# Interleaving two tensors: which queue opens with which load, and a tiny first write left out

## The chip, the cores and the metric

The kernel runs on one core of a Trainium2 chip. The metric is the time of one execution on the device, in microseconds (us); of several runs the median is taken. A hardware profile of one execution stands beside the times.

## The reference

The inputs x and y are float32 tensors of 32 x 256 x 1024, 33.5 MB each. The output has twice as many elements in its last dimension: x at the even places, y at the odd ones.

```python
result = np.zeros((batch, seq, dim * 2), dtype=np.float32)
result[..., 0::2] = x
result[..., 1::2] = y
```

Nothing is calculated. 67.1 MB have to be read and 67.1 MB to be written.

## The kernel before, in words

All three tensors are taken as flat arrays. The inputs are cut into eight pieces of 128 x 8192 elements (`WL = 8192`), so a piece of x or y is 4.19 MB, 32 KB in each of the 128 partitions of SBUF. For each piece the loop at L50 loads an x tile (L56) and a y tile (L57), both issued from SyncE (SP). Then, for each half of the piece (`WS = 4096` columns, the loop at L60), VectorE copies the half of x into the even columns of an output tile (L70) and the half of y into its odd columns (L71). The output tile, 128 x 8192 elements and again 4.19 MB, is stored by a DMA that ScalarE (ACT) issues (L72). So there are 16 loads of 4.19 MB, 32 copies and 16 stores of 4.19 MB.

The pools for x, y and output tiles have two buffers each (L35 to L37). A load of piece k+2 waits until the copies out of piece k are done; a copy into an output tile waits until the store from two before has landed. The waits and the order on each engine are made by the tile framework.

Two queues carry the DMAs: the profile calls SP's q1 and ACT's q10. Before, q1 holds all loads and q10 all stores. DMAs of a queue are taken in order of issue.

Two things concern the opening. At L44 to L47 a zero tile of 16 x 128 elements is made by VectorE and written by ACT to 16 places in the output that the first store overwrites later. And after compiling, L86 to L104 take the first DMA that SP issues (the load of the first x tile) out of the body and put it into the program's first block, ahead of SP's drain, with which the opening barrier of the engines begins. Every other DMA is issued after that barrier.

In what follows x0 and y0 are the tiles of the first piece, x1 and y1 those of the second, and so on.

Of the kernel before, what the change touches and what calls it, by code (L numbers as in the profile page):

```python
# [2 lines left out]

# [4 lines left out]


@with_exitstack
def _interleave(
    ctx: ExitStack,
    tc: tile.TileContext,
    x: bass.AP,
    y: bass.AP,
    out: bass.AP,
):
    nc = tc.nc
    P = 128  # L20

    total = 1
    for s in x.shape:
        total *= s

    WL = 8192
    WS = 4096

    xf = x.rearrange("b s d -> (b s d)")
    yf = y.rearrange("b s d -> (b s d)")  # L30
    of = out.rearrange("b s d -> (b s d)")

    fp32 = mybir.dt.float32

    xpool = ctx.enter_context(tc.tile_pool(name="xp", bufs=2))  # L35
    ypool = ctx.enter_context(tc.tile_pool(name="yp", bufs=2))
    opool = ctx.enter_context(tc.tile_pool(name="op", bufs=2))  # L37

    lwidths = [WL] * (total // P // WL)
    assert sum(lwidths) == total // P  # L40


    wpool = ctx.enter_context(tc.tile_pool(name="wp", bufs=1))
    zero = wpool.tile([16, 128], fp32, name="zero")  # L44
    nc.vector.memset(zero, 0.0)  # L45
    first = dataclasses.replace(of, offset=0, ap=[[2 * WL, 16], [1, 128]])
    nc.scalar.dma_start(out=first, in_=zero)  # L47

    start = 0
    for lw in lwidths:  # L50
        xtile = xpool.tile([P, WL], fp32, name="xtile")[:, :lw]
        ytile = ypool.tile([P, WL], fp32, name="ytile")[:, :lw]

        xs = dataclasses.replace(xf, offset=start, ap=[[lw, P], [1, lw]])
        ys = dataclasses.replace(yf, offset=start, ap=[[lw, P], [1, lw]])
        nc.sync.dma_start(out=xtile, in_=xs)  # L56
        nc.sync.dma_start(out=ytile, in_=ys)  # L57

        soff = 0
        while soff < lw:  # L60
            width = min(WS, lw - soff)
            otile = opool.tile([P, 2 * WS], fp32, name="otile")[:, : 2 * width]
            os_ = dataclasses.replace(
                of,
                offset=2 * start + 2 * soff,
                ap=[[2 * lw, P], [1, 2 * width]],
            )
            xsub = xtile[:, soff : soff + width]
            ysub = ytile[:, soff : soff + width]
            nc.vector.tensor_copy(out=otile[:, 0::2], in_=xsub)  # L70
            nc.vector.tensor_copy(out=otile[:, 1::2], in_=ysub)  # L71
            nc.scalar.dma_start(out=os_, in_=otile)  # L72
            soff += width

        start += P * lw
    assert start == total


def kernel(tc, x, y, out):
    nc = tc.nc  # L80
    _interleave(tc, x, y, out)
    tc.close()
    tc.compile()  # L83


    blocks = nc.main_func.blocks  # L86
    opening = blocks[0].instructions
    at, moved = next(
        (b, i)
        for b in blocks[1:]  # L90
        for i in b.instructions
        if i.engine == mybir.EngineType.SP and i.opcode == "DMACopy"
    )
    assert not moved.sync_info.on_wait
    body = at.instructions
    body.remove(moved)
    gate = next(
        n
        for n, i in enumerate(opening)
        if i.engine == mybir.EngineType.SP and i.opcode == "Drain"  # L100
    )
    opening.insert(gate, moved)
    at.instructions = body
    blocks[0].instructions = opening  # L104


# [1 line left out]
_INS = ['x', 'y']  # L108
_OUTS = [((32, 256, 2048), 'float32')]


# [23 lines left out]
```

## Time and profile before

| | |
|---|---|
| Median of 3 runs | 315.92 us (315.55 to 316.17) |
| Time of the profiled execution | 315.62 us |
| Span in its profile | 313.8 us |
| VectorE busy | 72.8 us (23%) |
| Moved | 134.23 MB, mean 428 GB/s |
| Loads on q1, stores on q10 | 67.11 MB, 67.12 MB |

The span runs from the first to the last instruction; 1.8 us of the execution lie around it. "Busy" counts VectorE's and GpSimd's work, not the issuing of DMAs. A group's line in the profile has the line of the kernel, the engine and operation, the tiles, the count, then busy time and mean time of one, then how long the engine stood idle before and what ended the wait. A line of the timeline has start, duration, engine, line and operation; where several are merged ("x3"), the duration runs from the first to the last. A line of the windows has the stretch, its length, busy time of VectorE and GpSimd, a clock that is of no use here, the busy share of the 16 DMA engines, and GB/s. The trace also has a record of every DMA packet, with its start, duration and size; a data packet of a tile is one row of 32 KB.

### The profile page before, as it was taken

The numbers are of one execution on the slowest core, as the hardware profiler recorded it, in microseconds if no ns is written. First come the engines' busy times: TensorE is split into PE (matmuls) and PEld (weight loads), VectorE is DVE, ScalarE is ACT, GpSimd is POOL, SyncE is SP. The second block draws the span as 40 slices with busy tenths as digits, with TensorE's granted clock in tenths as the row PEclk, the third lists the DMA queues.
The fourth block names the chain that finished last, engine by engine and source line by source line (L and its number), as shares of the span: only waits on it lengthen the run. The fifth ranks groups of instructions, "written<-read, shape, count | busy, mean of one in ns | idle before, by whom it ended". The sixth has DMA issues, their size and how long they took to land.

```text
span 313.8 us, 152 instructions
## 1 busy us (share of the span) xinstructions
DVE 72.8 (23%) x33; POOL 0.2 (0%) x4
## 2 busy tenths in 40 slices
DVE  0433002231032410325003150130501305023500
POOL 0000000000000000000000000000000000000000
DMA  8999999999999999999999999999999999999997
GB/s 339 464 405 397 468 401 464 405 464 405 464 405 464 405 459 409 451 418 451 418 434 434 430 439 426 443 413 455 401 468 401 468 401 468 401 468 401 464 405 334
DMA packets 4640, 134.23 MB, mean 428 GB/s; under 512 B 528, under 2 KB 544, under 8 KB 544
## 3 DMA queue, kind: packets, MB, share of 16 engines
q1 hardware_dynamic: 2304, 67.11, 49.9%
q10 hardware_dynamic: 2336, 67.12, 49.5%
HBM read 67.11 MB, written 67.12 MB: 428 GB/s over the span
## 4 chain that ended last, share of the span: by engine, by line
DMA 83%; DVE 11%; DVEq 1%; issue 0%
DMA out_dram<-otile 76%; DMA ytile<-in_y_dram 7%; DVE otile L71 6%; DVE otile L70 5%; DVEq L83 1%; DVEq L70 0%
## 5 line engine op out<-in xcount | busy, mean ns | idle before, releaser
L70 DVE COPY otile<-xtile 128x4096 f32<-128x4096 f32 x16 | 36.6, 2295 | 184.9 <-DMA out_dram<-otile 173.7
L71 DVE COPY otile<-ytile 128x4096 f32<-128x4096 f32 x16 | 36.6, 2292 | 39.8 <-DMA ytile<-in_y_dram 39.8
L45 DVE MEMSET zero<- 16x128 f32 x1 | 0.2, 165 | 0.9 <-PEq L119 0.9
L119 POOL MEMSET const-bfloat16-1.0<- 128x1 bf16 x1 | 0.1, 102 | 0.0
L119 POOL MEMSET const-uint8-127<- 128x1 uint8 x1 | 0.1, 102 | 0.0
L119 POOL MEMSET const-float32-0.0<- 128x1 f32 x1 | 0.1, 99 | 0.2 <-issue 0.2
L119 POOL MEMSET const-float32-1.0<- 128x1 f32 x1 | 0.1, 99 | 0.0
## 6 DMA issues: line engine op xcount, KB each, us to landing
out_dram<-otile ACTq DMA_DIRECT2D x16, 4096.0 KB, 29.1
xtile<-in_x_dram SPq DMA_DIRECT2D x8, 4096.0 KB, 43.6
ytile<-in_y_dram SPq DMA_DIRECT2D x8, 4096.0 KB, 60.7
out_dram<-zero ACTq DMA_DIRECT2D x1, 8.0 KB, 6.3
```

The costliest lines, as they stand in the source:

```text
L45: nc.vector.memset(zero, 0.0)
L70: nc.vector.tensor_copy(out=otile[:, 0::2], in_=xsub)
L71: nc.vector.tensor_copy(out=otile[:, 1::2], in_=ysub)
L83: tc.compile()
L119: nc = _bacc.Bacc("TRN2", target_bir_lowering=False, num_devices=1)
```

## The change

The zero tile, its memset and its write are gone. y0 is issued from ACT instead of SP. At the first turn of the loop the loads of the second piece are issued too: x1 from SP, the half of y1 in partitions 0 to 63 from ACT, and the half in partitions 64 to 127 from SP. The second turn finds its tiles in `held` and issues no loads. So q1 opens with x0, x1 and half of y1; q10 opens with y0 and the other half of y1, and the stores come after those. All later loads are on SP, all stores on ACT, as before.

The move ahead of the barrier is done for both engines: the first DMA of SP (x0) and the first of ACT (y0) go ahead of the drain of their engine. The rest of the diff writes the same copies and stores in another form.

```diff
-    wpool = ctx.enter_context(tc.tile_pool(name="wp", bufs=1))
-    zero = wpool.tile([16, 128], fp32, name="zero")
-    nc.vector.memset(zero, 0.0)
-    first = dataclasses.replace(of, offset=0, ap=[[2 * WL, 16], [1, 128]])
-    nc.scalar.dma_start(out=first, in_=zero)
+    def rows(flat, at, width, count=P):
+        return dataclasses.replace(flat, offset=at, ap=[[width, count], [1, width]])
...
+    held = None
+    for t, lw in enumerate(lwidths):
+        if held is None:
+            xtile = xpool.tile([P, WL], fp32, name="xtile")
+            ytile = ypool.tile([P, WL], fp32, name="ytile")
+        else:
+            xtile, ytile = held
+            held = None
...
+        if t != 1:
+            nc.sync.dma_start(out=xtile, in_=rows(xf, start, lw))
+            yq = nc.scalar if t == 0 else nc.sync
+            yq.dma_start(out=ytile, in_=rows(yf, start, lw))
+        if t == 0:
+            nxt = start + P * lw
+            nx = xpool.tile([P, WL], fp32, name="xtile")
+            ny = ypool.tile([P, WL], fp32, name="ytile")
+            nc.sync.dma_start(out=nx, in_=rows(xf, nxt, lw))
+            nc.scalar.dma_start(out=ny[:H], in_=rows(yf, nxt, lw, H))
+            nc.sync.dma_start(out=ny[H:], in_=rows(yf, nxt + H * lw, lw, P - H))
+            held = nx, ny
...
-    opening = blocks[0].instructions
-    at, moved = next(
-        (b, i)
-        for b in blocks[1:]
-        for i in b.instructions
-        if i.engine == mybir.EngineType.SP and i.opcode == "DMACopy"
-    )
...
+    for engine in (mybir.EngineType.SP, mybir.EngineType.Activation):
+        opening = blocks[0].instructions
+        at, moved = next(
+            (b, i)
+            for b in blocks[1:]
+            for i in b.instructions
+            if i.engine == engine and i.opcode == "DMACopy"
+        )
...
+            if i.engine == engine and i.opcode == "Drain"
```

More of the change, by code (lines that the diff above doesn't have):

```diff
@@ L40, in _interleave @@
     assert sum(lwidths) == total // P
-    wpool = ctx.enter_context(tc.tile_pool(name="wp", bufs=1))
-    zero = wpool.tile([16, 128], fp32, name="zero")
-    nc.vector.memset(zero, 0.0)
-    first = dataclasses.replace(of, offset=0, ap=[[2 * WL, 16], [1, 128]])
-    nc.scalar.dma_start(out=first, in_=zero)
-    start = 0
[L50 to L62, printed above, removed]
+    H = P // 2
+    def rows(flat, at, width, count=P):
+        return dataclasses.replace(flat, offset=at, ap=[[width, count], [1, width]])
+    start = 0
+    held = None
[18 more added lines that the diff above has]
+            held = nx, ny
+        for soff in range(0, lw, WS):
+            otile = opool.tile([P, 2 * WS], fp32, name="otile")
             os_ = dataclasses.replace(
@@ L65, in _interleave @@
                 offset=2 * start + 2 * soff,
-                ap=[[2 * lw, P], [1, 2 * width]],
+                ap=[[2 * lw, P], [1, 2 * WS]],
             )
[L68 to L71, printed above, removed]
+            nc.vector.tensor_copy(
+                out=otile[:, 0::2], in_=xtile[:, soff : soff + WS]
+            )
+            nc.vector.tensor_copy(
+                out=otile[:, 1::2], in_=ytile[:, soff : soff + WS]
+            )
             nc.scalar.dma_start(out=os_, in_=otile)
-            soff += width
         start += P * lw
@@ L86 @@
     blocks = nc.main_func.blocks
-    opening = blocks[0].instructions
-    at, moved = next(
-        (b, i)
-        for b in blocks[1:]
-        for i in b.instructions
-        if i.engine == mybir.EngineType.SP and i.opcode == "DMACopy"
-    )
[L94 to L104, printed above, removed]
+    for engine in (mybir.EngineType.SP, mybir.EngineType.Activation):
[5 more added lines that the diff above has]
+            if i.engine == engine and i.opcode == "DMACopy"
+        )
+        assert not moved.sync_info.on_wait
+        body = at.instructions
+        body.remove(moved)
+        gate = next(
+            n
+            for n, i in enumerate(opening)
+            if i.engine == engine and i.opcode == "Drain"
+        )
+        opening.insert(gate, moved)
+        at.instructions = body
+        blocks[0].instructions = opening
 _INS = ['x', 'y']
```

## The prediction

> **What bounds the kernel now.** First the page: busy time, the row of DMA shares, the queues, the groups.
>
> ```profile
> DVE 72.8 (23%) x33; POOL 0.2 (0%) x4
> ...
> DMA  8999999999999999999999999999999999999997
> ...
> DMA packets 4640, 134.23 MB, mean 428 GB/s; under 512 B 528, under 2 KB 544, under 8 KB 544
> ...
> q1 hardware_dynamic: 2304, 67.11, 49.9%
> q10 hardware_dynamic: 2336, 67.12, 49.5%
> ...
> L70 DVE COPY otile<-xtile 128x4096 f32<-128x4096 f32 x16 | 36.6, 2295 | 184.9 <-DMA out_dram<-otile 173.7
> L71 DVE COPY otile<-ytile 128x4096 f32<-128x4096 f32 x16 | 36.6, 2292 | 39.8 <-DMA ytile<-in_y_dram 39.8
> ```
>
> VectorE works 23% of the span; the 16 DMA engines are busy in every slice but the edges. VectorE waits 173.7 us for stores, so the chain of waits names stores (76%). But those stores wait for the DMA engines, which share their time between q1 (SP, loads) and q10 (ACT, stores). Next the timeline of the opening, to see who feeds them:
>
> ```profile
> 0.00 0.37 SPq L56 DMA_DIRECT2D xtile<-in_x_dram  x1
> ...
> 0.78 0.33 SPq L57 DMA_DIRECT2D ytile<-in_y_dram  x1
> 0.86 0.17 DVE L45 MEMSET zero<- 16x128 f32 x1 [0.86 <-PEq L119]
> 1.06 0.42 ACTq L47 DMA_DIRECT2D out_dram<-zero  x1
> 1.16 0.42 SPq L56 DMA_DIRECT2D xtile<-in_x_dram  x1
> 1.63 0.51 SPq L57 DMA_DIRECT2D ytile<-in_y_dram  x1
> 12.28 4.50 DVE L70 COPY otile<-xtile 128x4096 f32<-128x4096 f32 x2 [11.25 <-DMA xtile<-in_x_dram]
> 16.80 0.33 SPq L56 DMA_DIRECT2D xtile<-in_x_dram  x1
> 22.00 4.50 DVE L71 COPY otile<-ytile 128x4096 f32<-128x4096 f32 x2 [5.22 <-DMA ytile<-in_y_dram]
> 24.32 33.66 ACTq L72 DMA_DIRECT2D out_dram<-otile  x3
> ```
>
> By 2.14 us four loads (16.8 MB) stand in q1. x0 releases VectorE at 12.28, y0 at 22.00: 9.72 us for one 4.19 MB tile, with one queue at work, is 432 GB/s. One queue alone fills the engines. Last, windows, for where the rate falls short:
>
> ```profile
> 0.00:4.00 4.00, 0.17 (x1) 0.20 (x4) 1.00 0.78 262
> 4.00:24.00 20.00, 6.50 (x3) 0.00 (x0) 1.00 1.03 444
> 24.00:32.00 8.00, 2.50 (x2) 0.00 (x0) 1.00 1.00 397
> 32.00:288.00 256.00, 57.15 (x26) 0.00 (x0) 1.00 1.00 432
> 288.00:312.00 24.00, 6.47 (x3) 0.00 (x0) 1.00 1.01 437
> ```
>
> The last column is GB/s, the one before it the DMA share. The engines are busy throughout; the rate sags in two places only, the first 4 us and 24 to 32 us. (A window counts a packet where it starts, so edges wobble.) The packet records say what a slot is: a row of 32 KB takes 1.213 us on one engine. A 128-row tile is 8 rows on each of 16 engines, so the whole is 8x2 loads and 16 stores of 8 rows: 256 slots, 256 x 1.213 = 310.5 us. The first packet starts at 0.99 and needs 2.05 us (median of 16), so the cadence starts in effect at 1.84; 1.84 + 310.5 = 312.4. The last record ends at 312.71. The difference is the second sag: load packets in flight between 25.9 and 29.1, just ahead of the first big store's, take up to 1.9 us instead of 1.21. From rates spread evenly over each record (406.7 and 390.4 GB/s in the two 4 us windows from 24, against 433.3) it is (26.6 + 42.9) x 4 / 433.3 = 0.64 us. After the last packet come 1.14 us to the span's end at 313.85, and 1.77 us lie around the span (315.62). So time is won or lost only by idle slots, longer slots, or the two sags.
>
> [...] 433 GB/s with q1 alone, with both, and with q10 alone. [...] No 64-row transfer is in this trace. [...]
>
> **The change, part by part.**
>
> *y0 goes from SP's queue to ACT's, and both x0 and y0 are issued ahead of the barrier.* Rows of the two queues alternate, so x0 and y0 both end after some 16 slots: 1.84 + 16 x 1.213 = 21.2 us, plus about 0.7 us to release (x0 before: 11.54 to 12.28), some 21.9, as y0 does now (22.00). The early x0 copies are lost: VectorE does four copies of 2.3 us after 21 us, the first store leaves between 25.5 and 28 us instead of at 24.32. Nothing idles meanwhile: with y1's first half, q10 holds 12 slots a engine and q1 20. Cost 0; the cover is those 32 slots (38.8 us, until about 40). ACT's issue (0.4 us) ahead of its drain may hold the barrier a little and with it x1's issue (now 1.16); 16 slots, 19.4 us, are queued by then. POOL's queue has only its four constants. Cost 0.
>
> *The tiny write and its memset go.* One 512 B packet of 0.027 us on each engine, and VectorE's 0.17 us, which nothing waits for: gain 0.03 us. What it may have done for the first store is a rival below. The count of transfers stays 33, since y1 becomes two.
>
> *ACT's queue order.* y0 and half of y1 stand ahead of the stores. They wait for nothing. q10 has 12 rows an engine ahead of store 0, which ends them at slot 24: 1.84 + 29.1 = 30.9 us. The store's descriptors, issued by 28, then follow others in the same ring instead of opening it at 29.1. If the 0.64 us sag is the price of opening the ring, it goes or hides in the opening; if it belongs to the first large write, it stays. Between 0 and -0.64; I take half, -0.32.
>
> *SP's queue.* x1, then y1's second half, 20 slots, drain at about slot 40 (50 us); x2 is issued when x0's copies are done, before 28 us, y2 before 31. Neither queue runs dry. Later each store pair alternates as before: a store lands, two copies take 4.6 us, and the other store has 9.7 us or more to run. Cost 0.
>
> *y1 in two halves of 64 partitions.* The unknown. [...] The upper half-tile in q1 or the lower in q10, each has four slots an engine. First half (partitions 0 to 63), alternating with x1's rows: [...] +4 x 1.213 = 4.85 us, in any phase. Second half, alternating with store rows, which read SBUF: [...] +4 x (1.213 - offset between them). In perfect opposition that is 0. But the engines march nearly in step (store rows start within 0.43 us, at 29.10 to 29.53)[...]; I take 0.05 us, so 4 x 1.163 = 4.65. Sum 9.50. Bounds 0 (no limit) and 9.70; I take 9.50[...]. DMA slots are the path that sets the end, so all of it arrives there.
>
> Sum on the profiled execution: 315.62 + 9.50 - 0.32 - 0.03 = 324.77. The runs' median is 0.30 above this execution, so 325.1.
>
> **The rivals.** *Even slots, sag stays* (a tile half costs nothing, or its rows go to eight engines each, in balance; the sag is the first write's): 315.92 - 0.03 = 315.9, no change. For it: all records but those two groups are 1.213 us. [...] *Even slots, sag gone:* 315.92 - 0.64 - 0.03 = 315.25, faster. This is the case on the other side: its place is 25.9 to 29.1 us, its price 0.64 us, and it decides if a 64-row slot takes under 1.213 + 0.64/8 = 1.29 us and ring opening causes the sag. For it: only packets just ahead of q10's first large ones are long, and no later switch of queues costs anything. Against: the tiny write opened q10 at 5.27 with load rows beside it still at 1.213. *A colder first store:* the tiny write paid something for the first HBM write, and without it the store's first rows take what x0's took, +0.84 us: 316.8, slower. For it: x0's opening packets. Against: the sag occurs despite the tiny write.
>
> **How the numbers follow.** [...] 0.54 (own range 320.1 to 326.0: 315.92 + 4.85 - 0.64 to 315.92 + 9.70 + 0.4), even slots with the sag 0.18, without it 0.18, a colder store 0.10. A change under 0.2% (0.63 us) can't be told from none here. Slower 0.64, same 0.18, faster 0.18. Likeliest 325.1; the range, 315.1 to 326.0, reaches over all four, since leaving out the fast two would leave out 0.36.
>
> **What would show it.** Right: between some 21 and 31 us, and again between 45 and 60, the rate in the windows falls to about two thirds of 433 GB/s, and half-tile packets take near 2.4 us; later windows stay at 432; the last load ends some 9 us later; VectorE's first copies start near 21 us and DMA never idles. Wrong: half-tile rows at 1.21 us and a span within 1 us of 313.8; then the window 24 to 32 tells which rival holds. Idle DMA after 50 us would refute the queue count.

## The result, and the profile after

| | before | after |
|---|---|---|
| Median of 6 runs each, us | 316.02 (315.55 to 316.50) | 325.14 (324.81 to 325.88) |
| Profiled execution, us | 315.62 | 325.32 |
| Its span, us | 313.8 | 323.5 |
| Start to end of all data packets, us | 0.99 to 312.71 | 1.02 to 322.39 |

The changed kernel takes 1.029 of the time of the kernel before (95% interval 1.0275 to 1.0305). 9.7 us are added in the profiled executions, and almost all of it (9.65 us) lies between the first and the last packet.

From the page of the changed kernel, busy time, packets, queues and groups:

```profile
DVE 71.9 (22%) x32; POOL 0.2 (0%) x4
...
DMA  9999999999999999999999999999999999999997
...
DMA packets 4624, 134.22 MB, mean 415 GB/s; under 512 B 528, under 2 KB 528, under 8 KB 528
...
q10 hardware_dynamic: 2528, 73.40, 54.0%
q1 hardware_dynamic: 2096, 60.82, 45.4%
...
L79 DVE COPY otile<-xtile 128x4096 f32<-128x4096 f32 x16 | 36.7, 2295 | 236.1 <-DMA out_dram<-otile 169.9
```

The bytes and the copies are the same, and the DMA engines are as busy as before, in every slice, yet the mean rate is 415 GB/s instead of 428. Engines that are as busy and move less have rows that take longer. ACT's queue, q10, now carries 73.40 MB instead of 67.12, the 6.29 MB of y0 and half of y1.

The timeline of the opening of the changed kernel shows that what was moved went where it was meant to:

```profile
0.00 0.37 SPq L60 DMA_DIRECT2D xtile<-in_x_dram  x1
0.11 0.38 ACTq L62 DMA_DIRECT2D ytile<-in_y_dram  x1
...
0.92 0.33 SPq L67 DMA_DIRECT2D xtile<-in_x_dram  x1
0.92 0.51 ACTq L68 DMA_DIRECT2D ytile<-in_y_dram  x1
1.29 0.54 SPq L69 DMA_DIRECT2D ytile<-in_y_dram  x1
21.72 2.29 DVE L79 COPY otile<-xtile 128x4096 f32<-128x4096 f32 x1 [21.72 <-DMA xtile<-in_x_dram]
...
26.25 40.44 ACTq L85 DMA_DIRECT2D out_dram<-otile  x3
```

The barrier costs nothing: SP's first DMA behind it leaves at 0.92 instead of 0.78, but that is now x1, which before was the second and left at 1.16. VectorE starts at 21.72 instead of 12.28, the first store leaves at 26.25 instead of 24.32, and neither leaves the DMA engines idle. In both queues the DMAs land in the order in which they were issued: on SP x0 at 21.70, x1 at 46.44 and y1's upper half at 61.50; on ACT y0 at 21.87, y1's lower half at 39.13 and the first store at 61.69. In the opening the rows of the two queues alternate in waves of 16, which begin at 1.02 (SP), 2.78 (ACT), 4.00 (SP) and 5.20 us (ACT).

Windows of the changed kernel, cut where its rate changes (last column GB/s):

```profile
4.00:20.00 16.00, 0.00 (x0) 0.00 (x0) 1.00 1.03 444
22.00:38.00 16.00, 8.62 (x4) 0.00 (x0) 1.00 1.01 262
38.00:46.00 8.00, 0.00 (x0) 0.00 (x0) 1.00 1.07 459
46.00:60.00 14.00, 0.00 (x0) 0.00 (x0) 1.00 0.98 307
60.00:300.00 240.00, 58.46 (x26) 0.00 (x0) 1.00 1.00 433
```

and the same windows of the kernel before, but for the first:

```profile
22.00:38.00 16.00, 4.50 (x2) 0.00 (x0) 1.00 1.03 426
38.00:46.00 8.00, 0.00 (x0) 0.00 (x0) 1.00 0.91 393
46.00:60.00 14.00, 4.59 (x2) 0.00 (x0) 1.00 1.04 449
60.00:300.00 240.00, 59.02 (x26) 0.00 (x0) 1.00 1.00 433
```

Two stretches are slower than before and no other is. From 22 to 38 us, y1's lower half alternates with x1's rows: 262 GB/s. From 46 to 60 us, y1's upper half alternates with the first stores: 307. The packet records price them. Against 1.213 us a row, in the first stretch the half-tile rows take 2.25 us on average and x1's rows 1.80, together 6.46 us more on the mean engine (the sum of all excess, divided by 16). In each wave 16 half-tile rows are in flight at once, as many as there are DMA engines, and every one of them is slow (1.96 to 2.48 us). In the second, loads and stores together are 3.83 us over. That is 10.29 us. The opening row takes 0.52 us over its slot instead of 0.70, and the sag ahead of the first store, 0.64 us before, is 0.05. So 10.29 - 0.18 - 0.59 = 9.52 us are added on the mean engine; the last packet ends 9.68 us later.

### The profile page after: what moved, and what is told of

It reads as the page before. It is cut to its first block, busy times and chain, and to the rows that moved or that the text cites. A ratio compares the mean times of both kernels' runs of the same rounds, so it can differ in the third digit from the quotient of the medians.

```text
span 323.5 us, 151 instructions
## 1 busy us (share of the span) xinstructions
DVE 71.9 (22%) x32; POOL 0.2 (0%) x4
## 3 DMA queue, kind: packets, MB, share of 16 engines
q10 hardware_dynamic: 2528, 73.40, 54.0%
## 4 chain that ended last, share of the span: by engine, by line
DMA 75%; issue 10%; DVE 10%; DVEq 1%
DMA out_dram<-otile 68%; DMA xtile<-in_x_dram 7%; DVE otile L79 5%; DVE otile L82 5%; DVEq L95 1%; DVEq L79 0%
```

## The experiments

The theory: the rows of a load into partitions 0 to 63, or 64 to 127, take about twice as long, whoever issues it. That was the author's assumption; what such rows would wait for, no trace shows. The rivals are other parts of the change: loads ahead of the stores on ACT's queue, sharing y1 between queues, or the missing tiny write. Each kernel is timed against the kernel before on the same chip; "excess" is the time of rows over 1.213 us, on the mean engine.

**One part of the change alone: y1 in halves, in the kernel before.**

```diff
-        nc.sync.dma_start(out=ytile, in_=ys)
+        if start == P * lw:
+            for r in (0, P // 2):
+                part = dataclasses.replace(
+                    yf, offset=start + r * lw, ap=[[lw, P // 2], [1, lw]]
+                )
+                nc.sync.dma_start(out=ytile[r : r + P // 2], in_=part)
+        else:
+            nc.sync.dma_start(out=ytile, in_=ys)
```

> The kernel before with one edit: y1 is loaded as partitions 0 to 63, then 64 to 127, both from SP. No other part of the change is there. [...] y1's 8 slots take twice 1.213 us, +9.7 us: 325.7 us, with rows of about 2.43 us between 31 and 56 us (less [...]: down to +4.9, 320.9 us). Queues or the opening as the cause: 316.0 us and rows of 1.21 us.

Measured: 323.94 us, 1.0252 of before (1.0234 to 1.0270). Its windows from the sag of the first store to the end of the slow stretch:

```profile
22.00:34.00 12.00, 4.32 (x2) 0.00 (x0) 1.00 1.00 410
35.00:62.00 27.00, 2.30 (x1) 0.00 (x0) 1.00 1.02 324
62.00:300.00 238.00, 56.17 (x25) 0.00 (x0) 1.00 1.00 433
```

The split by partitions alone brings most of the loss, with both halves on SP, the tiny write in place and nothing moved. The excess after the sag is 7.4 us for eight slots, 0.93 each; half-tile rows reach 2.2 us, and the store rows between them take up to 1.47. The last packet ends 8.2 us later than before, 0.9 us more than the rows of the mean engine explain; less than half of that is because the engines end less together.

**The rest of the change alone: y1 whole, from SP.**

```diff
-            nc.scalar.dma_start(out=ny[:H], in_=rows(yf, nxt, lw, H))
-            nc.sync.dma_start(out=ny[H:], in_=rows(yf, nxt + H * lw, lw, P - H))
+            nc.sync.dma_start(out=ny, in_=rows(yf, nxt, lw))
```

> The changed kernel with y1 whole, from SP: ACT's queue opens with y0 alone. [...] no slow stretch, 315.2 us if the sag at the first store goes because ACT's queue holds a large load before it, 315.8 us if the sag comes back (q10 has drained y0 at 21 us and the first store leaves at 26, so the ring may stand empty for some 5 us). If opening ACT's queue with a load is what costs, above 320 us.

Measured: 316.02 us, ratio 1.0002 (0.9994 to 1.0010). No slow stretch: y0 on ACT, both early loads and the missing tiny write cost nothing together. They gain nothing either: the opening row has 0.57 us of excess instead of 0.70, but the sag is longer, 1.40 us.

**Shared by columns.** The two lines of y1 become two transfers over all 128 partitions, with rows of 16 KB:

```diff
-            nc.scalar.dma_start(out=ny[:H], in_=rows(yf, nxt, lw, H))
-            nc.sync.dma_start(out=ny[H:], in_=rows(yf, nxt + H * lw, lw, P - H))
+            C = lw // 2
+            for q, c in ((nc.scalar, 0), (nc.sync, C)):
+                part = dataclasses.replace(yf, offset=nxt + c, ap=[[lw, P], [1, C]])
+                q.dma_start(out=ny[:, c : c + C], in_=part)
```

> y1 is still shared between the two queues, two slots' worth each, but cut by columns: each part spans all 128 partitions. If the 64-partition halves are what costs [...], all rows run at full rate, the two slow stretches (22 to 38 and 47 to 61 us) vanish, and the opening's gain is left alone: 316.0 - 0.6 (no sag at the first store) - 0.2 (earlier opening) = 315.2 us. If instead sharing y1 between the queues, or loads ahead of the stores on ACT's queue, is what costs, it stays at about 325 us.

Measured: 316.11 us, ratio 1.0004 (0.9995 to 1.0012). Sharing y1 between the queues isn't the cause. The hoped-for 315.2 is refuted here as well. (This rests on the times of the runs alone.)

**64 rows on other partitions: even and odd.**

```diff
-            nc.scalar.dma_start(out=ny[:H], in_=rows(yf, nxt, lw, H))
-            nc.sync.dma_start(out=ny[H:], in_=rows(yf, nxt + H * lw, lw, P - H))
+            for q, r in ((nc.scalar, 0), (nc.sync, 1)):
+                part = dataclasses.replace(
+                    yf, offset=nxt + r * lw, ap=[[2 * lw, H], [1, lw]]
+                )
+                q.dma_start(out=ny[r::2], in_=part)
```

> The changed kernel with y1 cut into even partitions (ACT) and odd partitions (SP): again 64 rows each[...]. If the row count of 64 were the cause, 325 us. [...] 315.2 us [...]; if each engine takes four neighbouring rows of the 64, [...] about 325 us. [...]

Measured: 315.75 us, ratio 0.9986 (0.9979 to 0.9992), 9.4 us less than the changed kernel, with transfers of the same size, count, rows and queues. Its windows, cut as those of the changed kernel (the first is left out):

```profile
22.00:38.00 16.00, 8.78 (x4) 0.00 (x0) 1.00 1.03 426
38.00:46.00 8.00, 0.00 (x0) 0.00 (x0) 1.00 0.94 406
46.00:60.00 14.00, 4.50 (x2) 0.00 (x0) 1.00 1.02 442
60.00:300.00 240.00, 58.46 (x26) 0.00 (x0) 1.00 1.00 433
```

262 has become 426 and 307 has become 442. Every row of y1 takes 1.213 us; the sag (0.77 us) falls on rows of x1. So transfers of 64 rows, four to an engine, aren't slow as such: it matters which rows they are. One thing was still open: even and odd rows also lie differently in HBM.

**The same rows in HBM, other partitions.**

```diff
-            nc.scalar.dma_start(out=ny[:H], in_=rows(yf, nxt, lw, H))
-            nc.sync.dma_start(out=ny[H:], in_=rows(yf, nxt + H * lw, lw, P - H))
+            nc.scalar.dma_start(out=ny[0::2], in_=rows(yf, nxt, lw, H))
+            nc.sync.dma_start(out=ny[1::2], in_=rows(yf, nxt + H * lw, lw, P - H))
```

> y1's rows 0 to 63 in HBM go to the even partitions, rows 64 to 127 to the odd ones; the HBM side is that of the changed kernel, only the partitions differ. (y's rows of the second piece thus stand in other rows of the output than the reference has them.) If the partitions make the slow rows, 315.8 us as with even and odd rows; if the HBM side does, 325 us.

Measured: 315.71 us, ratio 0.9991 (0.9984 to 0.9998). The windows of the two slow stretches:

```profile
22.00:38.00 16.00, 8.73 (x4) 0.00 (x0) 1.00 1.03 424
...
46.00:60.00 14.00, 4.50 (x2) 0.00 (x0) 1.00 1.02 442
```

The HBM side is that of the changed kernel, and the loss is gone. So the cause is on the SBUF side: it is the partitions that a half of the rows goes to. With partitions 0 to 63 and then 64 to 127 the two stretches run at 262 and 307 GB/s, with even and then odd ones at 424 and 442. What the rows of a contiguous half wait for is in no record.

**The price of a half-tile row alone: x0 in halves,** both from SP, in the kernel before (the edit is that of y1, at `start == 0`).

> The kernel before with x0 loaded as partitions 0 to 63, then 64 to 127, both from SP: eight half-tile slots an engine with nothing else in flight. [...] rows take 2.43 us: +8 x 1.213 = +9.7 us, 325.9 us. [...] 2.69 us a row: +11.8 us, 328.0 us. If part of a row hides behind its neighbour, as where halves alternate with stores (0.93 us a slot), +7.5 us, 323.6 us.

Measured: 325.83 us, 1.0308 of before (1.0292 to 1.0324). Its windows:

```profile
4.00:20.00 16.00, 0.00 (x0) 0.00 (x0) 1.00 1.00 207
...
24.00:32.00 8.00, 3.46 (x2) 0.00 (x0) 1.00 1.07 459
```

With nothing but half-tiles in flight the core loads 207 GB/s. The rows take 2.56 us (median), 2.11 times 1.213. The excess of rows up to 24 us is 10.8 us, of which the opening has 0.7 in the kernel before too. The first packet comes 0.33 us later, and the sag at the first store, 0.64 us before, is 0.06 here: 10.1 + 0.33 - 0.58 = 9.85 us, the 9.9 us measured. The first of the three values was met, but with rows of 2.56 us, not the 2.43 that it assumed.

**Opposite halves in the two queues.** In the changed kernel x1 is cut too, upper half first:

```diff
-            nc.sync.dma_start(out=nx, in_=rows(xf, nxt, lw))
+            nc.sync.dma_start(out=nx[H:], in_=rows(xf, nxt + H * lw, lw, P - H))
+            nc.sync.dma_start(out=nx[:H], in_=rows(xf, nxt, lw, H))
```

> The changed kernel with x1 in halves too, upper half first: y1's lower half on ACT now alternates with x1's upper half on SP[...]. After that x1's lower half and y1's upper half follow on SP, each alternating with stores, where four slots cost 3.8 us before: 7.6 us together. If the engines march in step, every engine is at the lower half in one slot and at the upper in the next, each row takes about 2.56 us as with x0 in halves, and the first stretch costs 8 x 1.35 = 10.8 us: 316 + 18.4 = 334 us. If engines fall into opposition, the first stretch costs nothing: 323.5 us.

Measured: 332.69 us, 1.0523 of before (1.0496 to 1.0549). Its windows:

```profile
20.00:44.00 24.00, 8.90 (x4) 0.00 (x0) 1.00 1.02 240
44.00:80.00 36.00, 4.50 (x2) 0.00 (x0) 1.00 0.99 364
80.00:300.00 220.00, 49.45 (x22) 0.00 (x0) 1.00 1.00 433
```

The rows of the two queues together go to both halves of the partitions, and still they take 2.36 us. The 16 engines start their rows of one half within 1.3 us of each other and all turn to the other half after that. This fits the expectation that they march in step, but 1.3 us is more than half a row, and what the rows wait for isn't in the records: the reason is argued, not shown. The first stretch costs 10.5 us of excess. The second costs 5.8 us instead of 7.6, which makes up most of the distance to 334.

**The sag.** Three runs ask what sets the 0.64 us that the prediction hoped to save. y1 whole from ACT (the line of the second experiment with `nc.scalar`):

> The changed kernel with y1 whole, from ACT: the first store's rows stand behind 16 slots of loads on ACT's queue, its start moves to about slot 32 (41 us). All rows span 128 partitions: 316.0 us [...]. The sag at the first store was 0.77 us with half of y1 ahead on ACT (even and odd partitions) and 1.40 us with an empty ACT queue; a sag of 0.6 to 0.8 us here means that a filled queue keeps it short, 1.4 us that it doesn't.

Measured: 317.79 us, ratio 1.0059 (1.0039 to 1.0079); the sag is 0.66 us. Most of the 1.8 us have another place, which none of the theories had. ACT's queue holds two whole loads and SP's too few, so SP's runs empty from 79 to 88 us: x3 can't be issued before x1's copies are done at 83.27. When its rows begin at 88, loads and stores have long rows; from 80 to 100 us the excess is 1.5 us. Its timeline and a window there:

```profile
80.97 2.30 DVE L78 COPY otile<-xtile 128x4096 f32<-128x4096 f32 x1 [15.02 <-DMA out_dram<-otile]
...
83.29 0.33 SPq L60 DMA_DIRECT2D xtile<-in_x_dram  x1
```

```profile
84.00:96.00 12.00, 1.86 (x2) 0.00 (x0) 1.00 0.98 371
```

The kernel before without the tiny write:

```diff
-    wpool = ctx.enter_context(tc.tile_pool(name="wp", bufs=1))
-    zero = wpool.tile([16, 128], fp32, name="zero")
-    nc.vector.memset(zero, 0.0)
-    first = dataclasses.replace(of, offset=0, ap=[[2 * WL, 16], [1, 128]])
-    nc.scalar.dma_start(out=first, in_=zero)
```

> The kernel before without the tiny write and its memset, nothing else. If the tiny write paid part of the first store's cost, the long rows just before the first store add up to 1.3 to 1.4 us instead of 0.64, and the time is 316.1 + 0.7 = 316.8 us. If it is idle work, 316.1 us and a sag of 0.64 us.

Measured: 316.44 us, ratio 1.0007 (0.9997 to 1.0016); the sag is 0.73 us. The runs fall into two groups, about 315.6 and 316.5, and no difference from before can be told. The sag is 0.09 us longer, less than the 0.14 us by which two executions of one kernel differ (0.77 and 0.91, even and odd partitions). So no part of the sag is shown to be the tiny write's.

Even and odd partitions, with the tiny write from SP behind x0:

> The changed kernel with y1 in even and odd partitions, and the tiny write back, now issued from SP behind x0. If the tiny write shortens the sag, 0.77 us goes towards 0.6 or less and the time is 315.5 to 315.7 us; if it does nothing in this arrangement, 315.75 us as without it.

Measured: 315.91 us, ratio 0.9998 (0.9990 to 1.0006); the sag is 0.64 us. The tiny write brings nothing here.

**Is this version better than both?** Even and odd partitions without the tiny write, once more:

> The version with y1 in even and odd partitions once more, against the kernel before alone: 0.999 of it if the first comparison (0.9986, 0.9979 to 0.9992) holds, 1.000 if that was between chips or days.

Measured: 315.78 us, ratio 0.9990 (0.9984 to 0.9997). Twice the interval lies below 1. It is clearly faster than the changed kernel, but the gain on the kernel before is 0.1%, under the 0.2% that the prediction set as the least that can be told from no change. The best runs are no better: those of before go from 315.57 to 316.78, those of this version from 315.57 to 315.97. What it lacks is the slower part of before's runs; why, no trace shows.

## Why the prediction was right

The direction, the cause and the size hold: 325.1 us were predicted, 325.14 measured. That it came so close is luck: three terms of the sum are mis-sized, by +1.61, -0.82 and -0.45 us, and nearly cancel.

- *What bounds the kernel* holds. The DMA engines are 90% busy or more in every slice of the changed kernel but the last, and what its rows take longer arrives at the end (9.52 us on the mean engine, 9.68 at the last packet).
- *The free edits* hold: barrier, issue order, VectorE's later start, the missing memset. The kernel with y1 whole from SP has them all, and takes 1.0002 of the time before.
- *y1's halves* is right in its cause, half of the partitions; why such rows are slow isn't shown. Predicted were 4.85 + 4.65 = 9.50 us, both the author's estimates, on an assumption that no trace shows; measured were 6.46 + 3.83 = 10.29. The first half was too low: the half-tile rows are 4.13 us over their slots, and x1's rows another 2.33. All 16 x1 rows that follow a wave of half-tile rows take between 1.55 and 2.19 us. The second half was too high: with stores between, a slot costs 0.93 to 0.96 us, not 1.16. The traces show the store rows lengthened too, to 1.39 us on average, but not why.
- *March in step*, on which the second half rested, holds only at its beginning. The 16 half-tile rows of a wave start within 0.39 us of each other in the first of the four slots, within 0.59, 0.95 and 1.63 us in the next three, and take 2.04, 2.02, 1.96 and 1.90 us. The prediction kept an offset of 0.05 us. How much of the smaller cost comes from this isn't shown.
- *Opening ACT's queue early, -0.32*, is right in sign and wrong in reason. In the changed kernel the sag is gone (0.05), but not because the queue was open: with a filled queue and full-rate rows it was 0.64 to 0.91 us. Only where half-tile rows had been slow before the first store was it missing, here and with x0 in halves. So the term was -0.77 us (0.59 of the sag, 0.18 of the opening row), and the larger part comes with the slow rows: no full-rate version has it.
- *Rivals.* Slow half-tile rows, which the prediction held likeliest at 0.54, are what came. Even slots, with or without the sag, are refuted by the two slow stretches. Even slots without the sag is not to be had by opening the queue: no full-rate version lost it. The colder first store is refuted by the tiny write taken out alone: 0.09 us more sag, not 0.84, and a ratio of at most 1.0016, which is 0.5 us.
- *What would show it.* The two stretches came at 22 to 38 and 46 to 60 us at about the rate named, with half-tile rows of 2.25 and 1.98 us on average where the prediction had some 2.4. The last load ends at 293.34 instead of 287.29, 6.1 us later, not 9: with the even and odd split, at full rate, it ends at 283.71, 3.58 us earlier than before, probably since 12 rows of each engine's loads have left SP's queue. 283.71 and the 9.68 us added are 293.39. The prediction left out the first part.
- *Own time and median.* The profiled sum was 324.77, the execution 325.32; the runs after lie 0.18 us below their profiled one, where those of before lay 0.40 above. Half a microsecond of the agreement is luck of that kind.

## What to carry to other kernels

If a tile has to be split over two DMAs, cut it by columns or take every second partition, which cost nothing here (316.11 and 315.75 us); contiguous partition halves ran at 207 GB/s where whole tiles have 433, and two queues with opposite halves reached 240. When DMA engines are busy throughout and the rate still drops, look at single rows in the stretch where it drops. An edit to the order of the queues brought nothing here (ratio 1.0002 with y1 whole from SP), where one queue alone already fills the engines (432 GB/s).

## What was not expected

- Half-tile rows alone take 2.56 us, not twice 1.213 (2.43). With opposed halves in the two queues, rows are 2.36.
- The sag at the first store is 0.64 to 0.91 us, and 1.40 with y1 whole from SP. An empty ACT queue doesn't explain the 1.40: it was empty before the first store in the kernel before too, at 0.64. The sag is missing (0.05 and 0.06) where half-tile rows ran earlier, even when, with x0 in halves, these ended at 22 us and the first store's rows began at 38.6. What it is stays open: not the tiny write, not an unopened queue. A like loss (1.5 us) came when SP's queue had run empty and loads began again beside stores.
- 64 rows on even partitions ran at full rate (1.213 us a row), where the expectation was open: about 325 us if each engine takes four neighbouring rows. How the rows are dealt to the engines isn't in the records.
